# Mixture-of-experts stage: another order of issue for the transposes and evictions of the gated values

## The chip, the cores and the metric

The kernel runs on one core of a Trainium2 chip. The metric is the device time of one execution in microseconds. A measurement is the median of several runs; the trace is one profiled execution of the same program.

## What is computed

The reference is a two-layer transformer with mixers, one dense SwiGLU layer and, at the end, a mixture of 8 experts over 256 tokens of width 1024. The change lies in the mixture alone:

```python
def swiglu(h, w1, w3, w2):
    return (jax.nn.silu(h @ w1) * (h @ w3)) @ w2

def moe_swiglu(h, w_router, w1, w3, w2):
    logits = jnp.einsum('bnd,de->bne', h, w_router).astype(jnp.float32)
    top_vals, top_idx = lax.top_k(logits, TOP_K)          # 2 of 8
    gates = jax.nn.softmax(top_vals, axis=-1)
    ...
    for e in range(N_EXPERTS):
        out = out + combine[..., e:e + 1].astype(h.dtype) * swiglu(h, w1[e], w3[e], w2[e])
    return out
```

`w1[e]` and `w3[e]` are 1024 x 3584, `w2[e]` is 3584 x 1024, all in float32.

## The kernel before, in words

Experts are ordered by how many tokens they got. Even places (`small_(e)` false) are called big and take up to 128 tokens, odd ones small and take up to 64. An expert's 3584 inner columns are cut into 7 blocks of 512. The list `seq` orders the (expert, block) steps; but for its head and one stretch after the first big expert it alternates a big step and a small step, and such two together are called a **pair** here.

A float32 weight is not multiplied as it is. ScalarE copies a piece of 128 x 1024 into a rounded half `whi` (line 75), VectorE subtracts it into `wlo` (line 76), and TensorE multiplies both. These two instructions are a **split**; there are six buffers for split pieces, and `W.take()` prepares splits so far ahead that six are ready or in use. So the split of a piece can start when TensorE is done with the piece six places earlier. One quarter of a small step's `w1` and of its `w3` is used unsplit (line 1434).

Step i does the following:

- `hidden(p1, e)` and `hidden(p3, e)` multiply the tokens by the block of `w1` and of `w3`, four pieces each. For a big step (lines 1446 to 1448) the pieces are called **B1 to B4** (p1) and **B5 to B8** (p3) below, 6 matmuls each. For a small step (line 1438, 4 matmuls a piece) they are **S1 to S3** and **S4 to S6**, with the unsplit quarter behind S2 and behind S5.
- Between the two halves `turn(i - 1, prev, ...)` transposes the values of the step before: for a big one 4 transposes of `sl` (line 1477, called **T4**), then `gh` on ScalarE and `gl` on VectorE from PSUM; for a small one 8 transposes of two tiles `c` (line 1459, **T8**), then two `u` copies on ScalarE (1463), two `u` sums on VectorE (1464), Silu (1465), the product (1466), and the halves of `g`.
- After the second half, the values of this step leave PSUM: big, Silu on ScalarE and a product on VectorE into `sl` (1547, 1548); small, two copies `c` on ScalarE (1544).
- `finish(i - 1)` multiplies the turned values of the step before by four pieces of `w2`: **F1 to F4** for a small one (line 1493, 4 matmuls each), **G1 to G4** for a big one (line 1497, 6 each).

So a pair uses 22 split pieces in the order B1 to B8, F1 to F4, S1 to S6, G1 to G4, and the transfers of twelve raw tiles of 1024 KB, which SP issues in a ring of twelve. When an expert's last block is done, `rows` and `scatter` put its result back: products `po` into PSUM (1514, 1515), each evicted by VectorE into `xl` (line 400).

The order of each engine's queue is made by a scheduler, which lists what it thinks is ready sooner first. `tc.issue_after(m)` adds an edge without a wait: what is traced in its block goes behind m in the queue of the same engine. Before the change, the only such edges here are on the transposes: behind the sixth step of eight of the first half for a big step, behind the fourth for a small one (`TURN = (5, 3)`). They are traced after the whole half, and the copies and products have no edge.

Of the kernel before, what the change touches and what calls it, by code (L numbers as in the profile page):

```python
# [12 lines left out]
F32 = mybir.dt.float32  # L13
# [4 lines left out]
ALU = mybir.AluOpType  # L18
# [11 lines left out]
NF = EDIM // 512  # L30
EPS = 1e-6
RAW, RAW0, RAWF, RAW2, RAW3, WS, WS2 = 4, 5, 3, 5, 3, 3, 3
TURN = (5, 3)
FK = 7
KY = (2, 6)
QN = 4
# [11 lines left out]
def program(ctx, tc, a, out, upto=99, tap=None):  # L48
    nc = tc.nc
    V, S, G, TE = nc.vector, nc.scalar, nc.gpsimd, nc.tensor  # L50
# [21 lines left out]

    def split(hi, lo, full, eng=None):

        S.copy(hi, full)  # L75
        (eng or V).tensor_tensor(lo, full, hi.bitcast(F32), op=ALU.subtract)  # L76

    def mm3(o, wh, wl, xh, xl, first, last, **kw):
        TE.matmul(o, wh, xh, start=first, stop=False, **kw)  # L79
# [39 lines left out]
    class Stream:  # L119
# [20 lines left out]
        def prepare(self, n):  # L140
            while sum(lo is not None for _, lo in self.split_) < n and (self.ready or self.todo):
                self.fetch()
                t, whole = self.ready.popleft()
                if whole:
                    self.split_.append((t, None))
                    continue
                p = pairs.pop(0)
                pairs.append(p)
                hi = p.tile([P, 1024], F32R, tag="whi", name="whi")
                lo = p.tile([P, 1024], F32R, tag="wlo", name="wlo")  # L150
                split(hi, lo, t)
                self.split_.append((hi, lo))

        def take(self, ahead=None):
            ahead = self.ahead if ahead is None else ahead
# [3 lines left out]
    W = Stream(1)  # L159
# [7 lines left out]
    def small_(e):  # L167
        return e % 2 == 1
# [298 lines left out]
    with ExitStack() as st:  # L467
# [87 lines left out]
        u = mix.tile([P, 8], F32, name="u")  # L555
# [170 lines left out]
        po = bank("po")  # L726
# [693 lines left out]
    def experts(x0, then=None):  # L1420

        xg, py, gTs = {}, {}, {}

        def hidden(po, e):
            ms = []
            for q in range(4):
                wh, wl = W.take()
                if small_(e):
                    xs_, xf = (xg[e][n] for n in "sf")
                    for k2 in range(2):  # L1430
                        kt = 2 * q + k2
                        w = slice(512 * k2, 512 * (k2 + 1))
                        if wl is None:
                            m = TE.matmul(po[0:64], xf[:, kt], wh[:, w], start=False, stop=False, skip_group_check=True)  # L1434
                        else:
                            x_ = xs_[:, kt].rearrange("p u s -> p (u s)")
                            for z in (wh, wl):
                                m = TE.matmul(po, x_, z[:, w], start=kt == 0 and z is wh,  # L1438
                                              stop=kt == KT - 1 and z is wl, skip_group_check=True)
                        ms.append(m)  # L1440
                    continue
                xh, xl = xg[e]["h"], xg[e]["l"]
                for k2 in range(2):
                    kt = 2 * q + k2
                    w = slice(512 * k2, 512 * (k2 + 1))
                    TE.matmul(po, xh[:, kt], wh[:, w], start=kt == 0, stop=False)  # L1446
                    TE.matmul(po, xh[:, kt], wl[:, w], start=False, stop=False)  # L1447
                    m = TE.matmul(po, xl[:, kt], wh[:, w], start=False, stop=kt == KT - 1)  # L1448
                    ms.append(m)
            return ms  # L1450

        def turn_small(i, cs, m=None):

            pts = []
            with tc.issue_after(m.ins) if m else ExitStack():
                for c in cs:
                    pt = bank("pt")
                    for k in range(4):
                        TE.transpose(pt[:, P * k:P * (k + 1)], c[:, P * k:P * (k + 1)], ident)
                    pts.append(pt.rearrange("p (k u s) -> p k u s", k=4, u=2))  # L1460
            u = t512("u").rearrange("p (n k s) -> p n k s", n=2, k=4)
            for n, pt in enumerate(pts):
                S.copy(u[:, n], pt[:, :, 1])
                V.tensor_tensor(u[:, n], pt[:, :, 0], u[:, n], op=ALU.add)
            S.activation(u[:, 0], u[:, 0], AF.Silu)
            V.tensor_mul(u[:, 0], u[:, 0], u[:, 1])
            gT = t512("g").bitcast(F32R).rearrange("p (k u s) -> p k u s", k=4, u=2)
            split(gT[:, :, 0], gT[:, :, 1], u[:, 0])
            gTs[i] = gT

        def turn(i, sl, m=None):
            if small_(seq[i][0]):
                return turn_small(i, sl, m)
            pt = bank("pt")
            with tc.issue_after(getattr(m, "ins", m)) if m else ExitStack():
                for k in range(4):
                    TE.transpose(pt[:, P * k:P * (k + 1)], sl[:, P * k:P * (k + 1)], ident)
            gT = {n: t512(f"g{n}").bitcast(F32R).rearrange("p (k s) -> p k s", k=4) for n in "hl"}
            split(gT["h"], gT["l"], pt.rearrange("p (k s) -> p k s", k=4))
            gTs[i] = gT  # L1480

        def finish(i):
# [39 lines left out]
        prev = done = None  # L1522
        for i, (e, f) in enumerate(seq):
            p1, p3 = bank("p1"), bank("p3")
            ms = hidden(p1, e)
            if i == 0 and then:
                then()
            if i == QN:
                queue.clear()
            if i == 2 and not ids:  # L1530
                for j in range(1, EXP):
                    k = HP * (j % 2) + j // 2
                    ids[j] = nc.values_load(ords[0:1, k:k + 1].bitcast(I32), engines=[mybir.EngineType.SP],
                                            min_val=0, max_val=EXP - 1)
            if prev is not None:
                turn(i - 1, prev, ms[TURN[small_(e)]])
            if done:
                scatter(*done)
                done = None
            hidden(p3, e)  # L1540
            if small_(e):
                prev = [t512("c") for _ in range(2)]
                for c, po in zip(prev, (p1, p3)):
                    S.copy(c, po)  # L1544
            else:
                prev = t512("sl")
                S.activation(prev, p1, AF.Silu)
                V.tensor_mul(prev, prev, p3)
            if i == 0:
                one_hots(1)  # L1550
            if i == 1:
                xg[1] = gather(1)
            if f == NF - 1 and e < EXP - 2:
                xg[e + 2] = gather(e + 2)
            if i == len(seq) - 1:
                turn(i, prev)
            if i:
                finish(i - 1)
                if seq[i - 1][1] == NF - 1:
                    done = seq[i - 1][0], rows(seq[i - 1][0])  # L1560
            if f == 3 and e % 2 == 0:
                slots_back(e // 2)
            if f == 4 and e < EXP - 2:
                one_hots(e + 2)
# [108 lines left out]
```

## Time and profile before

| | us |
|---|---|
| median of 3 runs | 1800.47 (1798.79 to 1802.83) |
| profiled execution | 1802.29 |
| its span, first to last instruction | 1800.5 |
| TensorE busy | 1741.5 (97%) |
| VectorE busy | 1444.6 (80%) |
| ScalarE busy | 1039.4 (58%) |

The expert stage is about the second half of the span. Busy matmuls overlap each other in this profile, so TensorE's 97% does not say that it runs at its peak; distances between starts do. Where a row says what an engine waited for, that is the instruction whose end came last. A wait of an engine that is ahead costs nothing; what counts is where TensorE waits.

### The profile page before, as it was taken

The page shows a single profiled execution, that of the slowest core. Times are in us where ns is not written, and L with a number is a line of the kernel's source. Part 1 is how long each engine was busy: PE and PEld are TensorE (multiplying, and loading weights), DVE is VectorE, ACT ScalarE, POOL GpSimd, SP SyncE. Part 2 cuts the span into 40 slices and gives each one's busy share as a digit, 9 for nine tenths or more (in the row PEclk, how much of TensorE's full clock was granted, in tenths as well). Part 3 has the DMA queues.
Part 4 walks back from the last instruction along what each step waited for, and adds up shares of the span by engine and source line. Part 5 has one row for each costly group of instructions (what it writes and reads, how often), then busy time and mean ns, then how long its engine had stood idle before and what let it go on. Part 6 is the DMA issues. An engine that isn't in the chain of part 4 may idle for free.

```text
span 1800.5 us, 24070 instructions
## 1 busy us (share of the span) xinstructions
PE 1741.5 (97%) x8672; PEld 1365.1 (76%) x8672; DVE 1444.6 (80%) x2369; ACT 1039.4 (58%) x1425; POOL 7.4 (0%) x10
## 2 busy tenths in 40 slices
PE   6999999999999999999999999999999999999997
PEld 4778888888888899987777776766776777777675
DVE  5566599987554988877898888888888888988887
ACT  3353342222223455556787776777767777767775
POOL 0000000000000000000000000000000000000000
PEclk9999999999999999997999999999999999999999
DMA  8543554755212221176999899999989999899990
GB/s 364 187 165 121 228 211 178 276 201 192 112 54 88 94 71 71 52 292 237 351 374 402 349 327 359 394 362 383 364 310 361 373 391 369 326 365 378 378 387 34
DMA packets 65935, 474.12 MB, mean 263 GB/s; under 512 B 7312, under 2 KB 7696, under 8 KB 8464
## 3 DMA queue, kind: packets, MB, share of 16 engines
q1 hardware_dynamic: 65664, 472.31, 69.1%
q8 instruction: 70, 1.15, 0.3%
q14 instruction: 57, 0.47, 0.1%
q10 hardware_dynamic: 144, 0.20, 0.0%
HBM read 471.43 MB, written 1.05 MB: 262 GB/s over the span
## 4 chain that ended last, share of the span: by engine, by line
PE 80%; DVE 10%; ACT 4%; issue 4%; DMA 2%; DVEq 0%; SPq 0%; ACTq 0%
PE p L1438 9%; PE py L1497 8%; DVE wlo L76 6%; PE p L1434 5%; PE p L80 4%; PE p L81 4%; PE p L79 4%; PE p L1446 4%; PE p L1447 4%; PE p L1448 4%; PE po L79 3%; PE po L80 3%; PE po L81 3%; PE py L1493 3%; ACT whi L75 3%
## 5 line engine op out<-in xcount | busy, mean ns | idle before, releaser
L76 DVE TENSOR_TENSOR wlo<-raw,whi 128x1024 fp32r<-128x1024 f32 x738 | 873.0, 1221 | 142.9 <-ACT whi L75 133.8
L75 ACT CAST whi<-raw 128x1024 fp32r<-128x1024 f32 x738 | 741.8, 1049 | 365.4 <-PE p L80 157.4
L1446 PE MATMUL p<-whi,xh 128*128 128x512 f32 x448 | 178.0, 397 | 0.0
L1447 PE MATMUL p<-wlo,xh 128*128 128x512 f32 x448 | 175.5, 392 | 0.0
L1448 PE MATMUL p<-whi,xl 128*128 128x512 f32 x448 | 175.2, 391 | 0.0
L1438 PE MATMUL p<-whi,xs 128*128 128x512 f32 x336 | 141.6, 422 | 1.6 <-ACT c L1544 1.5
L1438 PE MATMUL p<-wlo,xs 128*128 128x512 f32 x336 | 136.7, 407 | 5.0 <-DVE wlo L76 5.0
L80 PE MATMUL p<-hlo,whi 128*128 128x512 f32 (+1 forms) x368 | 139.7, 381 | 0.2
L79 PE MATMUL p<-hhi,whi 128*128 128x512 f32 (+1 forms) x368 | 138.3, 381 | 1.1 <-ACT hhi L363 1.1
L81 PE MATMUL p<-hhi,wlo 128*128 128x512 f32 (+1 forms) x368 | 139.3, 380 | 0.0
L1434 PE MATMUL p<-raw,xf 128*64 128x512 f32 x224 | 108.1, 605 | 0.0
L1438 PEld LDWEIGHTS p<-whi,xs 128*128 128x128 f32 x336 | 63.7, 189 | 57.8 <-ACT whi L75 22.1
L1447 PEld LDWEIGHTS p<-wlo,xh 128*128 128x128 f32 x448 | 84.8, 189 | 18.3
L1446 PEld LDWEIGHTS p<-whi,xh 128*128 128x128 f32 x448 | 84.9, 190 | 17.3 <-ACT xh L75 0.2
L1448 PEld LDWEIGHTS p<-whi,xl 128*128 128x128 f32 x448 | 84.7, 189 | 17.5
L1497 PE MATMUL py<-wlo,gh 128*128 128x512 f32 x224 | 88.6, 396 | 0.1
L1497 PE MATMUL py<-whi,gl 128*128 128x512 f32 x224 | 88.7, 396 | 0.0
L1493 PE MATMUL py<-wlo,g 128*128 128x512 f32 x224 | 84.8, 411 | 3.7 <-DVE wlo L76 3.7
L1493 PE MATMUL py<-whi,g 128*128 128x512 f32 x224 | 83.9, 407 | 2.4 <-DVE g L76 0.9
L1438 PEld LDWEIGHTS p<-wlo,xs 128*128 128x128 f32 x336 | 63.8, 190 | 28.6 <-DVE wlo L76 18.6
L941 PE MATMUL pp<-wlo,hhi 128*128 128x256 f32 x288 | 81.8, 284 | 1.2 <-DVE wlo L76 1.2
L940 PE MATMUL pp<-whi,hhi 128*128 128x256 f32 x288 | 82.6, 287 | 0.0
(373 smaller groups left out, 3205.1 us busy)
## 6 DMA issues: line engine op xcount, KB each, us to landing
raw<-moe_w SPq DMA_DIRECT2D x335, 1024.0 KB, 7.3
raw<-ffn SPq DMA_DIRECT2D x33, 1024.0 KB, 4.9
raw<-w_mod SPq DMA_DIRECT2D x24, 1024.0 KB, 7.3
raw<-w_mod_t SPq DMA_DIRECT2D x24, 1024.0 KB, 4.9
raw<-w_in_odd SPq DMA_DIRECT2D x12, 1024.0 KB, 4.7
raw<-w_in_even SPq DMA_DIRECT2D x6, 1024.0 KB, 6.7
raw<-w_out_even SPq DMA_DIRECT2D x4, 1024.0 KB, 7.0
raw<-w_out_odd SPq DMA_DIRECT2D x4, 1024.0 KB, 4.8
```

Source lines behind the costliest of these rows:

```text
L75: S.copy(hi, full)
L76: (eng or V).tensor_tensor(lo, full, hi.bitcast(F32), op=ALU.subtract)
L79: TE.matmul(o, wh, xh, start=first, stop=False, **kw)
L80: TE.matmul(o, wh, xl, start=False, stop=False, **kw)
L81: TE.matmul(o, wl, xh, start=False, stop=last, **kw)
L1434: m = TE.matmul(po[0:64], xf[:, kt], wh[:, w], start=False, stop=False, skip_group_check=True)
L1438: m = TE.matmul(po, x_, z[:, w], start=kt == 0 and z is wh, stop=kt == KT - 1 and z is wl, skip_group_check=True)
L1446: TE.matmul(po, xh[:, kt], wh[:, w], start=kt == 0, stop=False)
L1447: TE.matmul(po, xh[:, kt], wl[:, w], start=False, stop=False)
L1448: m = TE.matmul(po, xl[:, kt], wh[:, w], start=False, stop=kt == KT - 1)
L1493: TE.matmul(py[e][n], gT[:, ft].rearrange("p u s -> p (u s)"), w[:, 512 * n:512 * (n + 1)], start=first and w is wh, stop=last and w is wl)
L1497: TE.matmul(py[e][n], gT[g][:, ft], w[:, 512 * n:512 * (n + 1)], start=first and g == "h" and w is wh, stop=last and g == "l")
```

## The change

Three things in the source. (1) The transposes are traced inside the first half, right behind its fourth step of eight (the end of its second quarter), for big and small steps alike: `TURN = 3`. (2) The `Stream` of weights remembers the two instructions of the split that it prepared last (`W.last`), and `W.then(k)` puts what follows behind it on ScalarE (k = 0) or VectorE (k = 1). (3) That is used for the `u` copies and sums, `gh` and `gl`, both `c` copies and the product `sl`. No instruction is added or taken away.

```diff
-TURN = (5, 3)
+TURN = 3
     def split(hi, lo, full, eng=None):
-        S.copy(hi, full)
-        (eng or V).tensor_tensor(lo, full, hi.bitcast(F32), op=ALU.subtract)
+        h = S.copy(hi, full)
+        return h, (eng or V).tensor_tensor(lo, full, hi.bitcast(F32), op=ALU.subtract)
...
-                split(hi, lo, t)
+                self.last = split(hi, lo, t)
...
+        def then(self, i=0):
+
+            return tc.issue_after(self.last[i].ins)
...
-        def hidden(po, e):
-            ms = []
+        def hidden(po, e, at=None):
...
-                    ms.append(m)
-            return ms
+                    if kt == TURN and at:
+                        at(m)
...
-                S.copy(u[:, n], pt[:, :, 1])
-                V.tensor_tensor(u[:, n], pt[:, :, 0], u[:, n], op=ALU.add)
+                with W.then():
+                    S.copy(u[:, n], pt[:, :, 1])
+                with W.then(1):
+                    V.tensor_tensor(u[:, n], pt[:, :, 0], u[:, n], op=ALU.add)
...
-            split(gT["h"], gT["l"], pt.rearrange("p (k s) -> p k s", k=4))
+            pv = pt.rearrange("p (k s) -> p k s", k=4)
+            with W.then():
+                S.copy(gT["h"], pv)
+            with W.then(1):
+                V.tensor_tensor(gT["l"], pv, gT["h"].bitcast(F32), op=ALU.subtract)
...
-            ms = hidden(p1, e)
+            hidden(p1, e, None if prev is None else lambda m: turn(i - 1, prev, m))
...
-            if prev is not None:
-                turn(i - 1, prev, ms[TURN[small_(e)]])
...
-                    S.copy(c, po)
+                    with W.then():
+                        S.copy(c, po)
...
-                V.tensor_mul(prev, prev, p3)
+                with W.then(1):
+                    V.tensor_mul(prev, prev, p3)
```

What it moves is told by the order of the built programs. ScalarE's queue before, in a pair in the middle of expert 2's blocks: the first row ends with the splits of B1 to B6, and the row under it is the two `u` copies.

```order
L75 CAST whi<-raw 128x1024 x8
L1463 COPY u<-pt 128x256 x2
L75 CAST whi<-raw 128x1024 x2
L1465 ACTIVATE u<-u 128x256
L75 CAST whi<-raw 128x1024
L75 CAST g<-u 128x4x64
L75 CAST whi<-raw 128x1024
L1547 ACTIVATE sl<-p_10914 128x512
L75 CAST whi<-raw 128x1024 x7
L75 CAST gh<-pt 128x512
L75 CAST whi<-raw 128x1024
L1544 COPY c<-p_11065 128x512
```

The same pair now (the lines of the new file are some four to twelve higher): the `c` copies stand behind B1, the `u` copies behind B7, `gh` behind G1.

```order
L1553 COPY c<-p_10795 128x512
L1553 COPY c<-p_10796 128x512
L75 CAST whi<-raw 128x1024 x6
L1468 COPY u<-pt 128x256 x2
L75 CAST whi<-raw 128x1024
L1471 ACTIVATE u<-u 128x256
L75 CAST whi<-raw 128x1024 x2
L75 CAST g<-u 128x4x64
L1556 ACTIVATE sl<-p_10914 128x512
L75 CAST whi<-raw 128x1024 x9
L1487 CAST gh<-pt 128x512
L75 CAST whi<-raw 128x1024 x4
```

Of the split rows, x2 became x1 ahead of Silu and x7 plus one became x9 ahead of `gh`. On TensorE T8 moved from behind B4 to behind B2 in all such pairs, and T4 from behind the first half of the small step to behind S2. On VectorE `sl` moved from behind F2 to behind S1.

One pair of the program before has another order than its neighbours, that of the second block of expert 4 (its T8 starts at 1347.04 us in the trace). On ScalarE the seven splits of its second row are B2 to B8, and the `u` copies stand behind them:

```order
L1544 COPY c<-p_12017 128x512
L75 CAST whi<-raw 128x1024 x7
L1463 COPY u<-pt 128x256 x2
L75 CAST whi<-raw 128x1024
L1465 ACTIVATE u<-u 128x256
L75 CAST whi<-raw 128x1024
L75 CAST g<-u 128x4x64
```

In this one the change leaves the `u` copies where they are, behind B8.

The program's end, on ScalarE before: behind the last small step's two `c` copies come its `u` copies (its T8 stands right behind S6 on TensorE, cut in two by three matmuls of G1).

```order
L1544 COPY c<-p_15745 128x512
L75 CAST whi<-raw 128x1024 x2
L1544 COPY c<-p_15746 128x512
L1463 COPY u<-pt 128x256 x2
L75 CAST whi<-raw 128x1024 x2
L1465 ACTIVATE u<-u 128x256
L75 CAST whi<-raw 128x1024
L75 CAST g<-u 128x4x64
```

The same place now; on TensorE the last T8 stands behind all matmuls of G1 to G4, and two splits and the Silu stand behind the `u` copies here.

```order
L1553 COPY c<-p_15745 128x512
L1553 COPY c<-p_15746 128x512
L75 CAST whi<-raw 128x1024
L1468 COPY u<-pt 128x256 x2
L75 CAST whi<-raw 128x1024 x2
L1471 ACTIVATE u<-u 128x256
L75 CAST g<-u 128x4x64
```

The last split of all stood behind `g` and now stands ahead of the Silu.

## Rows read from the trace of the kernel before

**Rows 1.** Chain that ended last, in time: start us, us, what.
```profile
1122.36 5.47 PE py L1497 x24
```

**Rows 2.** TensorE's timeline, T8 and T4: start us, us, engine, line, operation, count.
```profile
895.68 1.03 PE L1459 MATMUL pt<-const,c 128*128 128x128 f32 x8
...
928.50 1.03 PE L1459 MATMUL pt<-const,c 128*128 128x128 f32 x8
...
1100.15 1.03 PE L1459 MATMUL pt<-const,c 128*128 128x128 f32 x8
...
1266.12 1.04 PE L1459 MATMUL pt<-const,c 128*128 128x128 f32 x8
...
1347.04 1.03 PE L1459 MATMUL pt<-const,c 128*128 128x128 f32 x8
...
1362.01 0.60 PE L1477 MATMUL pt<-const,sl 128*128 128x128 f32 x4
...
1378.19 1.03 PE L1459 MATMUL pt<-const,c 128*128 128x128 f32 x8
...
1511.18 1.04 PE L1459 MATMUL pt<-const,c 128*128 128x128 f32 x8
...
1620.32 1.03 PE L1459 MATMUL pt<-const,c 128*128 128x128 f32 x8
...
1752.52 1.04 PE L1459 MATMUL pt<-const,c 128*128 128x128 f32 x8
...
1769.28 0.60 PE L1477 MATMUL pt<-const,sl 128*128 128x128 f32 x4
```

**Rows 3.** ScalarE's timeline in one pair; in brackets the idle time before, and its releaser.
```profile
1133.76 0.81 ACT L1463 COPY u<-pt 128x256 f32<-128x256 f32 x2 [3.19 <-PE pt L1459]
...
1140.03 6.73 ACT L75 CAST whi<-raw 128x1024 fp32r<-128x1024 f32 x7
1150.52 0.59 ACT L75 CAST gh<-pt 128x512 fp32r<-128x512 f32 x1 [3.76 <-PE pt L1477]
```

**Rows 4.** Waits from 800 us on: who waited for whom, us, times, longest.
```profile
ACT u L1463 <- PE pt L1459: 65.0, 25, 3.8
...
ACT whi L75 <- DMA raw<-moe_w: 0.6, 2, 0.3
```

**Rows 5.** VectorE's timeline in the same pair.
```profile
1134.16 0.86 DVE L1464 TENSOR_TENSOR u<-pt,u 128x256 f32<-128x256 f32 x2 [1.02 <-ACT u L1463]
...
1140.82 0.68 DVE L1548 TENSOR_TENSOR sl<-sl,p 128x512 f32<-128x512 f32 x1
1141.42 8.03 DVE L76 TENSOR_TENSOR wlo<-raw,whi 128x1024 fp32r<-128x1024 f32 x7
```

**Rows 6.** TensorE's timeline in the same pair.
```profile
1144.96 0.50 PE L1438 MATMUL p<-wlo,xs 128*128 128x512 f32 x1 [0.17 <-DVE wlo L76]
...
1149.88 0.60 PE L1477 MATMUL pt<-const,sl 128*128 128x128 f32 x4
```

**Rows 7.** TensorE's timeline where a result is put back.
```profile
1029.84 0.39 PE L1514 MATMUL po<-pT,yh 128*128 128x256 f32 x1 [1.50 <-ACT c L1544]
...
1554.62 0.39 PE L1514 MATMUL po<-pT,yh 128*128 128x256 f32 x1 [1.40 <-DVE xl L400]
```

**Rows 8.** Timelines of TensorE and VectorE at the end.
```profile
1774.56 0.60 PE L1459 MATMUL pt<-const,c 128*128 128x128 f32 x4
...
1781.43 0.42 DVE L76 TENSOR_TENSOR g<-u,g 128x256 fp32r<-128x256 f32 x1
```

**Rows 9.** Windows: busy us of each engine (instructions), TensorE's clock, transfer share, GB/s.
```profile
980.00:1000.00 20.00, 20.00 (x105) 17.03 (x104) 16.94 (x19) 15.64 (x19) 0.00 (x0) 1.00 1.01 417
...
1100.00:1200.00 100.00, 97.71 (x410) 69.11 (x409) 85.42 (x90) 73.98 (x91) 0.00 (x0) 1.00 0.98 376
```

More of the change, by code (lines that the diff above doesn't have):

```diff
@@ L1448, in hidden @@
                     m = TE.matmul(po, xl[:, kt], wh[:, w], start=False, stop=kt == KT - 1)
-                    ms.append(m)
-            return ms
+                    if kt == TURN and at:
+                        at(m)
         def turn_small(i, cs, m=None):
```

## The prediction, made before the changed kernel was timed

> **What bounds the kernel now.** I began with the page's shares, then asked who waits for whom in the expert stage (860 to 1800 us of the span), then laid the three engines' instructions of one pair of steps side by side in time. TensorE is the engine to follow: its 24 matmuls of a second product take 5.47 us [rows 1], that is 0.228 us each with nothing between them, so a quarter of a big half (6 matmuls) is 1.37 us and a quarter of a small step (4) is 0.91 us.
>
> The period of a pair is the distance from one group of eight transposes (of a small step's values; T8 below) to the next [rows 2]. From 1100.15 to 1266.12 five pairs take 165.97 us, from 1378.19 to 1511.18 four take 132.99, from 1620.32 to 1752.52 four take 132.20: about 33.0 each. But from 1347.04 to 1378.19 one takes 31.15, with the same instructions. So about 1.8 us of a pair is waiting, and it is not lost in every pair. That is what a change of order can win.
>
> Where it goes: ScalarE, in order, stands 3.19 us at the `u` copy until the transposes come, and 3.76 us at `gh` [rows 3]; in all it waits 65.0 us for T8 at the line of `u` [rows 4]. VectorE, which makes the second half of each split from ScalarE's first, stands behind it (1.02 us before its `u`) and then runs seven splits without a pause, 8.03 us or 1.15 each [rows 5]; in that stretch TensorE has caught up and waits for a `wlo` [rows 6]. The one unhurried pair differs in just this: in its order the `u` copies stand behind B8, in the slow ones behind B6 (both are shown with the change). Weights are not what is waited for: ScalarE waited 0.6 us in all for a weight transfer [rows 4].
>
> **The change, part by part.** The instructions are the same in number and kind on every engine, and SP's queue of transfers is the same, so only waits can move. I clock a pair from TensorE's first matmul of B1 = 0, all six split buffers full.
>
> (a) T8 goes from behind B4 to behind B2, and the `u` copies from behind the split of B6 to that of B7. TensorE: B1 and B2 to 2.73, T8 (1.03 us [rows 2]) to 3.8, B3 to 5.1, B4 to 6.5, B5 to B8 to 11.95, F1 to F4 to 15.6, S1 and S2 to 17.4. A split may begin when the piece six places earlier has been used. B7's buffer is free at 1.37, so its first half is done at 2.4. A copy follows its transposes' start by 0.64 us (1149.88 to 1150.52 [rows 3, 6]): the two `u` copies run from 3.4 to 4.2. ScalarE's wait there is about 1.0 us instead of 3.19. Then the splits by VectorE's 1.15 us, ScalarE's 0.96 (6.73 for seven [rows 3]) before them: B8 ready 6.4, product of `u` 6.8, F1 7.95, `g` 8.4, F2 9.5, F3 10.7, F4 11.8, S1 13.0 (its buffer comes free at 10.6). TensorE wants F1 and `g` at 11.95, F4 at 14.7, S1 at 15.6: everything is 2.5 us or more ahead, where before it was late.
>
> (b) `sl` moves behind S1's split on VectorE and T4 (the four transposes of a big step) ahead of the unsplit quarter: `sl` (0.68 us [rows 5]) ends at 13.7, S2 at 14.8; TensorE reaches S2 at 16.5 and T4 at 17.4. T4 stands in TensorE's own queue, so whatever `sl` lacks is paid there in full; the spare is 3.7 us.
>
> (c) `gh` moves behind G1 and both `c` copies behind the next B1. `gh` still waits for T4, but G1 to G4 are not wanted for another 8 us. The `c` copies wait for the end of S6, which the buffer of B2 waits for as well, so they add only their own time to a queue that is 4 us ahead. I put (c) at nothing; without that cover it would be 2 times 0.6 us a pair.
>
> The sum for steady pairs, at the unhurried period of 31.15: 165.97 - 5 x 31.15 = 10.22, 132.99 - 4 x 31.15 = 8.39, 132.20 - 4 x 31.15 = 7.60. Each run holds one pair with extra work on routing (transposes of `hot`), which a pair with the same extra shows as 928.50 - 895.68 = 32.82, so 1.67 comes off each: 8.55 + 6.72 + 5.93 = 21.2. The last pair's T8 to T4 is 16.76 against 14.97 in the unhurried one [rows 2]: 1.8. **Steady pairs: -23.0.** Bounds: 0 if the wait only changes places, -23 if all of it goes (the period cannot be shorter than the 31.15 by order alone, as far as rows show).
>
> (d) Where one expert's result is put back. At 1029.84 TensorE waits 1.50 for a `c` copy to free a PSUM bank [rows 7]; the new order puts five of the `xl` evictions ahead of the `u` work there, and the small step's second product no longer stands ahead of a half. I take -2 there. At the two later places (1.40 at 1554.62 [rows 7]) the evictions still stand behind `g`, and now all eight in a row: +0.5 each. Bounds for the three together: -4.5 (all such waits gone) to +4 (one more wait of 1.4 at each).
>
> (e) The end. The last T8 stood right behind S6; the order now has it behind all 24 matmuls of G1 to G4, 5.47 us later, with two splits and then the Silu behind the `u` copies. From S6's end (1774.56): 5.47 + 0.64 + 0.81 (copies) + 2 x 0.96 + 0.42 (Silu, taken as one more step like `g`) + 0.42 (product) + 1.15 (last split) + 0.42 (`g`) = 11.3; before, `g` ended at 1781.85, that is 7.3 [rows 8]. What follows (16 matmuls, sixteen evictions) was interleaved with three splits that are then already done, about 1 us. **+3**, bounds 0 (copies find cover) and +5.5 (the whole of G1 to G4).
>
> Sum: -23.0 - 2 + 1 + 3 = -21. The profiled execution took 1802.29 us, the span 1800.5 of it; so 1781.3 for it, and from the median of the three runs, 1800.47, which lies 1.8 below, **1779.5 us**.
>
> **A rule against it.** Twelve transfers of 1024 KB (12.58 MB) feed a pair. At 31.15 us that asks for 404 GB/s. The rows show 376 GB/s at a transfer share of 0.98 over 1100 to 1200, and 417 at 1.01 over 980 to 1000 [rows 9].
>
> The Trainium skill, "DMA: Bandwidth & Descriptors", section Where 436 GB/s comes from, gives about 358 GB/s as the limit of memory for one core and 435 for the ports, and says that for transfers from memory the 358 binds. By it no pair could be under 35.1 us and nothing would be won (1800 and a tail of 3). The trace disagrees, with 417 GB/s in [rows 9] and a pair of 31.15 us in [rows 2].
>
> **Rivals.** (1) *The weights become the bound.* For it: a share of 0.98 to 1.01. Against it: 417 GB/s over 20 us, and no waiting for weights in the row above. If the stage cannot hold more than 390 GB/s (half way between the 376 of the rows and the 404 asked for), a pair stays at 32.3 us, 0.7 x 14 = 10 us are won, less the 2 that (d) and (e) add: 1792. (2) *ScalarE's wait shrinks but does not go*, since the `u` copies move by a single split and still meet their transposes late. Half of 23 is left: -11.5 + 2, also 1791. For it: the one unhurried pair had them two splits later. Against it: T8 comes two quarters earlier as well. (3) *More goes than the steady waits*: the waits of (d) at all places, the end covered: -23 - 4.5 - 3 (the waits in the first pairs of an expert that I left out), about 1770. (4) *Slower: T4 comes too early.* Were VectorE to gain nothing, `sl` would end at 1140.82 + 0.68 + 3 x 1.15 = 1144.95, and T4 would stand some 4.6 us before 1149.88 (2.8 us of matmuls that it passes, 1.8 of waits), at 1145.3: a spare of 0.3 us. From there each microsecond by which VectorE is later is paid on TensorE in each of some 25 pairs: one split late (1.15) makes 0.85 x 25 = 21, with the end's 3, 1824. It decides from 0.3 us on; my clocking has 3.7.
>
> **How the numbers follow.** Forecast 0.64 (its own range 1774 to 1786, from the bounds of (d) and (e)); rival 1 0.12, rival 2 0.09, rival 3 0.09, rival 4 0.06. The range of 8 in 10 takes in rivals 1 to 3 and leaves out rival 4 and the far ends: 1770 to 1793. A measurement of this kernel can tell about 0.2% (3.6 us) from no change. Faster by more than that: the forecast, rival 3 and nearly all of rivals 1 and 2, 0.88; within it: the low ends of rivals 1 and 2, 0.05; slower: rival 4 and a little of (d), 0.07.
>
> **What would show it.** The distance between T8 groups is 31 to 31.5 in all steady pairs; ScalarE's wait at the `u` copy is near 1 us, its total a third of 65.0; VectorE's stretches without a pause no longer end in TensorE waiting for a `wlo`; T4 waits for nothing; the end from S6 on is about 3 us longer. It is wrong if T8 to T8 stays near 33 (which wait ends there tells rival 1, a transfer, from rival 2, a ScalarE copy), or if TensorE waits before T4 for `sl`.

## The result, and the profile after

The changed kernel took 1781.29 us (median of 4 runs, 1780.00 to 1783.31), the kernel before 1799.63 beside it: ratio 0.9893, 95% interval 0.9881 to 0.9906. Predicted were 1779.5. The profiled execution took 1780.0 us, its span is 1778.1.

Busy times of the page after: us, share of the span, instructions.

```profile
PE 1720.7 (97%) x8672; PEld 1373.6 (77%) x8672; DVE 1440.7 (81%) x2369; ACT 1050.1 (59%) x1425; POOL 7.4 (0%) x10
```

TensorE's share is 97% as before, though its busy time fell by 21 us, from 1741.5: the share said nothing about where the time was. TensorE's timeline does, by the starts of T8 (start us, us, engine, line, operation, count), as [rows 2] before. The first two are neighbours in the middle of expert 2, the other two lie around a putting back.

```profile
1090.64 1.03 PE L1463 MATMUL pt<-const,c 128*128 128x128 f32 x8
1121.59 1.03 PE L1463 MATMUL pt<-const,c 128*128 128x128 f32 x8
...
1286.47 1.03 PE L1463 MATMUL pt<-const,c 128*128 128x128 f32 x8
1329.65 1.03 PE L1463 MATMUL pt<-const,c 128*128 128x128 f32 x8
```

The pair is 30.95 us where it was 32.97. ScalarE's and VectorE's timelines of the same pair, as [rows 3, 5] (in brackets the idle time ahead and its releaser):

```profile
1122.22 0.81 ACT L1468 COPY u<-pt 128x256 f32<-128x256 f32 x2 [0.74 <-PE pt L1463]
...
1136.73 0.58 ACT L1487 CAST gh<-pt 128x512 fp32r<-128x512 f32 x1
...
1144.54 0.59 ACT L1553 COPY c<-p 128x512 f32<-128x512 f32 x1 [1.63 <-PE p L1441]
```

```profile
1127.20 4.65 DVE L76 TENSOR_TENSOR wlo<-raw,whi 128x1024 fp32r<-128x1024 f32 x4
1131.77 0.68 DVE L1558 TENSOR_TENSOR sl<-sl,p 128x512 f32<-128x512 f32 x1
1132.36 6.90 DVE L76 TENSOR_TENSOR wlo<-raw,whi 128x1024 fp32r<-128x1024 f32 x6
```

The wait at `u` is 0.74 us (before 3.19), that at `gh` is gone (before 3.76). In TensorE's timeline F1 to F4 now follow each other at 0.91 us a piece, S1 comes right behind them, and T4 stands there without a wait, 3.65 us after `sl` has ended (1131.77 + 0.68):

```profile
1130.65 0.39 PE L1503 MATMUL py<-whi,g 128*128 128x512 f32 x1
...
1134.28 0.39 PE L1441 MATMUL p<-whi,xs 128*128 128x512 f32 x1
...
1136.10 0.60 PE L1483 MATMUL pt<-const,sl 128*128 128x128 f32 x4
```

In such a pair no matmul has an idle time ahead of it any more: 30.95 us is what TensorE's own work takes at this order. Who waited for whom from 800 us on (us, times, longest), as [rows 4], and a window of two pairs (its length, busy us of PE, PEld, DVE, ACT, POOL, then clock, transfer share, GB/s), as [rows 9]:

```profile
ACT u L1468 <- PE pt L1463: 17.0, 18, 4.4
...
ACT whi L75 <- DMA raw<-moe_w: 1.5, 5, 0.3
```

```profile
1090.64:1152.54 61.90, 61.90 (x266) 46.24 (x264) 57.83 (x59) 50.33 (x60) 0.00 (x0) 1.00 1.00 408
```

The transfers kept up: 408 GB/s over 62 us, and 1.5 us of waiting for a weight in all. The rule that the prediction weighed (the Trainium skill, "DMA: Bandwidth & Descriptors", section Where 436 GB/s comes from) has about 358 GB/s as what binds transfers from memory; this row, with 408, disagrees.

Laid end to end by the starts of T8, the two traces give this (us; T8 is two quarters, 2.73 us, earlier in its pair now, which the first row gains and the last gives back):

| stretch | before | after | change | predicted |
|---|---|---|---|---|
| start to first T8 | 895.68 | 892.90 | -2.78 | -2.73 |
| three pairs, first expert | 95.50 | 94.23 | -1.27 | 0 |
| first putting back, with two neighbours | 108.97 | 103.51 | -5.46 | -2 |
| five pairs | 165.97 | 157.66 | -8.31 | -8.55 |
| second putting back | 80.92 | 81.35 | +0.43 | +0.5 |
| five pairs | 164.14 | 157.70 | -6.44 | -6.72 |
| third putting back | 77.98 | 81.09 | +3.11 | +0.5 |
| five pairs | 163.36 | 156.94 | -6.42 | -5.93 |
| last pair and end | 47.98 | 52.72 | +4.74 | +2.73 - 1.8 + 3 |
| span | 1800.5 | 1778.1 | -22.4 | -21 |

### The profile page after: what moved, and what is told of

It reads as the page before. It is cut to its first block, busy times and chain, and to the rows that moved or that the text cites. A ratio compares the mean times of both kernels' runs of the same rounds, so it can differ in the third digit from the quotient of the medians.

```text
span 1778.1 us, 24106 instructions
## 1 busy us (share of the span) xinstructions
PE 1720.7 (97%) x8672; PEld 1373.6 (77%) x8672; DVE 1440.7 (81%) x2369; ACT 1050.1 (59%) x1425; POOL 7.4 (0%) x10
## 3 DMA queue, kind: packets, MB, share of 16 engines
q8 instruction: 70, 1.15, 0.3%
## 4 chain that ended last, share of the span: by engine, by line
PE 90%; DVE 6%; ACT 1%; DMA 1%; issue 1%; SPq 0%; DVEq 0%; ACTq 0%
PE p L1441 9%; PE py L1507 9%; PE p L1437 6%; PE p L1450 5%; PE p L1451 5%; PE p L1452 5%; PE py L1503 5%; PE p L80 4%; PE p L81 4%; PE p L79 4%; PE po L79 3%; PE po L80 3%; PE po L81 3%; PE pg L1407 2%; DVE wlo L76 2%; PE pp L945 2%
## 5 line engine op out<-in xcount | busy, mean ns | idle before, releaser
L75 ACT CAST whi<-raw 128x1024 fp32r<-128x1024 f32 x738 | 752.1, 1050 | 427.2 <-PE p L80 157.4
L946 PE MATMUL pp<-whi,hlo 128*128 128x256 f32 x288 | 81.5, 283 | 0.0
L1503 PE MATMUL py<-wlo,g 128*128 128x512 f32 x224 | 81.2, 395 | 0.0
```

The source lines that it names most:

```text
L75: h = S.copy(hi, full)
L1503: TE.matmul(py[e][n], gT[:, ft].rearrange("p u s -> p (u s)"), w[:, 512 * n:512 * (n + 1)], start=first and w is wh, stop=last and w is wl)
```

## The experiments

Three ideas stood against each other. **D**, distance: an engine's queue runs in order, so a copy that waits for its transposes holds up the splits behind it, and what counts is how many splits stand in ScalarE's queue between the place of T8 and the copy; I call these the pieces **ready** at T8 (before: T8 behind B4, `u` behind B6, so 2; now T8 behind B2, `u` behind B7, so 5). **P**, place: the earlier transposes are the gain. **Rivals on cost**: which of the moved instructions carries it, or whether too few buffers or the weights do. The steady pair is the measure, since it repeats to about 0.1 us within a kernel (one pair of 32.26 in e6 aside); the medians also hold what happens where a result is put back, and the clock there.

| kernel | T8, `u` behind | ready | `sl` behind | steady pair, us | median, us |
|---|---|---|---|---|---|
| before | B4, B6 | 2 | F2 | 32.97 | 1799.5 to 1800.8 |
| e1, transposes alone | B2, B4 | 2 | F2 | 32.93 | 1795.40 |
| e8, seven buffers | B4, B6 | 2 | F2 | 32.92 | 1800.82 |
| e4, all edges but `u` | B2, B4 and B6 | 2 | S1 | 32.53 | 1805.41 |
| e3, `u` edges alone | B2, B7 | 5 | F2 | 32.02 | 1785.96 |
| e6, no edges on `c`, `sl` | B2, B7 | 5 | F2 | 31.88 | 1783.88 |
| e2, edges alone | B4, B8 | 4 | S1 | 31.14 | 1788.66 |
| e5, no edges on `gh`, `gl` | B2, B7 | 5 | S1 | 31.08 | 1785.15 |
| e9, no edges on `c` | B2, B7 | 5 | S1 | 31.05 | 1768.56 |
| e10, TURN = 1 | B1, B6 | 5 | S1 | 30.97 | 1779.54 |
| e11, TURN = 7 | B4, F1 | 5 | S1 | 30.97 | 1783.35 |
| changed kernel | B2, B7 | 5 | S1 | 30.95 | 1781.29 |

### Place or distance: e1, e2, e11, e10

e1 takes every `with W.then(...)` away and keeps the transposes where the change has them:

```diff
-                with W.then():
+                with ExitStack():
                     S.copy(u[:, n], pt[:, :, 1])
```

(and so at the other edges).

> Part (1) alone: the transposes stand where the change puts them (T8 behind B2, T4 behind S2), no copy or product has an edge. The scheduler answers by moving the copies along: `u` behind the split of B4 (before: B6, changed kernel: B7), `gh` behind S4. So each copy stands as near behind its transposes as before. Theory D (what counts is how many splits stand ahead of a copy in ScalarE's queue after its transposes are asked for, so that ScalarE has work until they come): nothing is won, pairs of 33.0 us (32.6 to 33.4), ScalarE's wait at `u` 55 to 75 us in all, 1800 (1794 to 1806). Theory P (the earlier place of the transposes is the gain, since `u`, `g` and F1 start earlier): pairs near 31, 1781 (1777 to 1786).

Measured: 1795.40, ratio 0.997 (0.9956 to 0.9984), pairs of 32.93, ScalarE's wait at `u` 46.0 us in all (theory D had 55 to 75). **The earlier transposes alone win nothing in a steady pair.** The 5 us that it is faster lie elsewhere: the first putting back takes 104.35 us, before 108.97, and most of that is the clock, whose mean there is 1.00 and was 0.97.

e2 is the reverse: `TURN = (5, 3)`, the turn traced behind the whole half as before, with the split that the half had prepared at its fourth step as the edge.

> Parts (2) and (3) alone: edges on the same splits as in the changed kernel, the transposes where they were before (T8 behind B4, T4 behind the first half of the small step). The scheduler then has `u` behind B8 (the order of the one unhurried pair of the kernel before), `gh` behind G2, `c` behind B1. Theory D: the gain is there without any move of the transposes: pairs of 31.0 us (30.9 to 31.4), wait at `u` under 30 us in all, 1781 (1776 to 1788). Theory P: pairs near 33, 1800 (1794 to 1806).

Measured: 1788.66, ratio 0.9925 (0.9898 to 0.9952), just above the range that D had (1788 at most); the pair is as D said. ScalarE's wait at `u` is not: 43.8 us in all where D had under 30, 2.10 in a steady pair, and the pair hardly pays for it. TensorE's timeline:

```profile
1101.27 1.03 PE L1463 MATMUL pt<-const,c 128*128 128x128 f32 x8
...
1132.41 1.03 PE L1463 MATMUL pt<-const,c 128*128 128x128 f32 x8
```

31.14 us with T8 in its old place: that is the 31.15 of the unhurried pair of [rows 2]. What it lacks beside the changed kernel lies in the steady stretches (478.5 against 472.3 us, half of it in the pairs with extra work, two of 34.8 and one of 34.6 against two of 33.9 and one of 33.1) and at the first putting back (107.91 against 103.51).

e11 and e10 change one number, `TURN`, to 7 and to 1.

> The changed kernel with the transposes as late as the kernel before had them: TURN = 7, T8 behind B4 and T4 behind the first half of the small step. The edges follow and put `u` behind F1 and `gh` behind G2. Theory D: five pieces are ready at T8 again, so pairs of 31.0 us (30.9 to 31.2) with T8 in its old place, unless the last half of `g` comes too late for F1 (clocked: `g` 0.5 to 1 us ahead of it, so a loss of up to 0.5 a pair is open: 31.4). 1781 to 1789. Theory P (place): 33.0, 1800.

> The changed kernel with the transposes one more quarter earlier: TURN = 1, so T8 stands behind B1 and T4 behind S1; the edges follow (`u` behind B6, `gh` behind S6). Theory D: five pieces stay ready at T8, as with TURN = 3, and `sl` has 3.7 us of spare in the changed kernel, of which a quarter of the small half takes 0.9: pairs of 30.95 (30.9 to 31.2), 1781 (1777 to 1786). The prediction's rival 4 (T4 too early, TensorE waits for `sl`): each pair 0.5 us or more longer, 1793 or more.

Measured: 1783.35, ratio 0.9898 (0.9874 to 0.9921), and 1779.54, ratio 0.987 (0.9842 to 0.9899). T8 of e11, at its old place behind B4, and its `u` copies behind F1 in ScalarE's timeline:

```profile
1098.97 1.03 PE L1463 MATMUL pt<-const,c 128*128 128x128 f32 x8
...
1129.94 1.03 PE L1463 MATMUL pt<-const,c 128*128 128x128 f32 x8
```

```profile
1130.57 0.81 ACT L1468 COPY u<-pt 128x256 f32<-128x256 f32 x2 [0.74 <-PE pt L1463]
```

30.97 us, and the same 0.74 us of wait at `u` as in the changed kernel. T8 behind B1, B2 or B4 gives the same pair as long as five pieces are ready. **Place is out, distance stands.**

The kernel before shows the same inside one trace. Counted there, its hurried pairs all have 2 pieces ready. The unhurried one at 1347.04 has 4, and there is a second like it, at 1589.16, also with 4, which takes 31.17 us; the pairs at 928.50 and 959.82 have 6 and take 31.32 and 31.36. e10 also tells that T4 a quarter earlier still finds `sl` done: the prediction's rival 4 has more room than the trace of before could show.

### Buffers or order: e8

```diff
-RAW, RAW0, RAWF, RAW2, RAW3, WS, WS2 = 4, 5, 3, 5, 3, 3, 3
+RAW, RAW0, RAWF, RAW2, RAW3, WS, WS2 = 4, 5, 3, 5, 2, 3, 4
```

in the kernel before.

> The kernel before, its order untouched (`u` behind B6, `gh` behind S5, T8 behind B4), with seven split buffers instead of six and eleven raw tiles instead of twelve. Theory D (the copy's place in ScalarE's queue sets how far ahead VectorE is at T8: B6 is ready and B7 is not, whatever the number of buffers): pairs stay at 32.97 (32.7 to 33.2), 1800 (1795 to 1804). Rival L (six buffers are too few, and the change only hides that): pairs fall to 31 to 32, 1785 (1778 to 1793). Rival W (the ring of weights is tight): pairs grow past 33.3, 1806 or more.

Measured: 1800.82, ratio 1.001 (0.9997 to 1.0024). T8, and ScalarE at `u`:

```profile
1094.74 1.04 PE L1459 MATMUL pt<-const,c 128*128 128x128 f32 x8
...
1127.66 1.04 PE L1459 MATMUL pt<-const,c 128*128 128x128 f32 x8
```

```profile
1128.30 0.81 ACT L1463 COPY u<-pt 128x256 f32<-128x256 f32 x2 [3.18 <-PE pt L1459]
```

32.92 us, and ScalarE stands 3.18 us at `u` (before 3.19), although a seventh buffer is there for the split behind it. **More buffers do not help where the order of the queue holds the work back.** The run changes two things, one buffer more and one raw tile less, but the unchanged wait at `u` says that no gain of the one is hidden by the other. Its two pairs with 6 pieces ready (T8 at 1343.10 and 1586.80) take 30.99 us. The Trainium skill ("PSUM — Partial Sum Buffer", section Engine vs sequencer instructions) calls the queues of ScalarE and VectorE strictly first in, first out; the 3.18 us of the row above agree.

The size can be clocked now, from the rows of before: T8 on TensorE, and the splits behind the `u` sums on VectorE.

```profile
1133.12 1.04 PE L1459 MATMUL pt<-const,c 128*128 128x128 f32 x8
...
1135.55 2.36 DVE L76 TENSOR_TENSOR wlo<-raw,whi 128x1024 fp32r<-128x1024 f32 x2 [0.52 <-ACT whi L75]
```

With 2 pieces ready, VectorE ends the `u` sums 1.9 us after T8's start (1134.16 + 0.86 in [rows 5], less 1133.12) and waits 0.5 for the next first half. From there to S2 it has eight splits of 1.15 (B7 to S2), two steps of `u` and `g` at 0.34 from start to start, and `sl` at 0.60: 10.5, so S2 is ready 12.9 us after T8's start. TensorE wants it after 0.79 + 5.47 + 3.64 + 0.91 = 10.8 (T8, B5 to B8, F1 to F4, S1). That is 2.1 us late; measured 32.97 - 30.95 = 2.02. With 4 ready two splits fall away, 2.3 us, and nothing is late; measured 0.19. This clocking has no wait at `sl`; the next runs show one as soon as `u` has been moved without it.

### Which moved instruction: e3 to e6, e9

> The changed kernel with the edges on the `u` copies and sums alone; `gh`, `gl`, `c` and the product `sl` are free, and the scheduler has `gh` behind S4 again (before: S5, changed: G1). Theory D in the form that the wait at `u` carries the gain and the wait at `gh` is covered (the prediction's (c)): `gh` waits 50 to 70 us in all again, and pairs are still 31.0 (30.9 to 31.5), 1782 (1777 to 1788). Theory H (both waits cost about alike, since before ScalarE stood 65.0 us at `u` and 68.4 at `gh`): pairs of 32 (31.7 to 32.4), 1791 (1787 to 1796).

Measured: 1785.96, ratio 0.9918 (0.9886 to 0.995), pairs of 32.02: half, as theory H said (the median lies in D's range and below H's), and `gh` waited 64.1 us. I took that to be `gh`'s doing. It was not.

> The opposite: edges on all but the `u` copies and sums. The scheduler has one `u` copy behind B4 and one behind B6, with T8 behind B2. Theory D with the wait at `u` as the carrier: no more than a small part of the gain, pairs of 32.5 to 33.2, 1797 (1791 to 1803). Theory H: half, 32 and 1791. Theory P: 31 and 1781.

Measured: 1805.41, ratio 1.0014 (0.9993 to 1.0034): unchanged at best and above what any of the three theories gave, though the pair is a little shorter (32.53, in D's range). ScalarE waits 87.1 us at `u`. Its pairs with extra work are longer, 35.1 against 34.1, so that the steady stretches win 1 us in all, and the last pair and end take 57.18 us (before 47.98, and 2.73 for the place of T8).

> The changed kernel without the edges on `gh` and `gl` alone: the scheduler has `gh` behind S4 again (as in e3), all else as in the changed kernel. After e3 the theory is: a copy that stands k splits behind the place of its transposes in TensorE's order lets VectorE be no more than k pieces ahead there, and what it lacks is paid in F1 to S2, where TensorE takes 0.91 us a piece and VectorE makes one in 1.15. Theory G (in e3 it was `gh` behind S4 that cost 1.1 us a pair): pairs of 32.0 us again (31.8 to 32.2), `gh` waits over 55 us in all; 1785 (1781 to 1790). Theory C (it was the product `sl` and the `c` copies): pairs of 30.95, 1779 (1775 to 1784).

Measured: 1785.15, ratio 0.9911 (0.9891 to 0.993). Its waits:

```profile
ACT gh L1487 <- PE pt L1483: 57.8, 17, 4.2
ACT u L1468 <- PE pt L1463: 16.7, 19, 3.8
```

`gh` waits 57.8 us in all (before 68.4), up to 4.2 at a time, and the pair is 31.08: **those waits cost 0.13 us a pair.** (In the traces of e1, e3 and e5 `gh` stands behind S3 in the steady pairs, one piece earlier than the expectations say; the median is a little above theory C's range.) I read it so: behind `gh` VectorE has the whole of G1 to G4 and B1 to B4, at 1.37 us a piece for TensorE against 1.15, to make it good. Theory G fell, and with it my reading of e3.

> The changed kernel without the edges on the `c` copies and the product `sl`: `gh` stays behind G1, the `c` copies go behind G2, `sl` behind F2. Theory G: pairs of 30.95 (30.9 to 31.1), 1781 (1777 to 1785). Theory C: pairs of 32.0, 1790 (1785 to 1795).

Measured: 1783.88, ratio 0.9901 (0.9884 to 0.9918), pairs of 31.88: by the pair, though not by the median, it is `c` or `sl`. e9 tells them apart, with `sl` kept on its edge:

```diff
                 for c, po in zip(prev, (p1, p3)):
-                    with W.then():
+                    with ExitStack():
                         S.copy(c, po)
```

> The changed kernel without the edges on the two `c` copies alone; `sl` keeps its own. ScalarE has both `c` copies behind G2 (changed kernel: behind the next B1), and the order where a result is put back becomes that of e6. Theory C now says: the second `c` copy waits for the end of S6 with only G1 and G2 split, and the pieces that are then late cannot all be made good until S2: pairs of 31.9 us (31.7 to 32.1), as in e6, and the second pair at each of the two later places of putting back 39.1 instead of 43: 1783 (1779 to 1787). Rival S (it was `sl` that stood too early on VectorE in e6): pairs of 30.95, 1772 (1768 to 1776).

Measured: 1768.56, ratio 0.9824 (0.98 to 0.9849), pairs of 31.05. My theory C was wrong, the rival right. VectorE's timeline of the same pair, e6 first, then e9:

```profile
1130.86 0.69 DVE L1558 TENSOR_TENSOR sl<-sl,p 128x512 f32<-128x512 f32 x1 [0.74 <-PE p L1452]
```

```profile
1132.48 0.67 DVE L1558 TENSOR_TENSOR sl<-sl,p 128x512 f32<-128x512 f32 x1
```

In e6 `sl` stands behind F2's split and VectorE waits 0.74 us for the last matmul of B8, with the splits that TensorE wants next behind it in the queue; in e9 it stands behind S1 and waits for nothing. The pairs differ by 0.83 us. In the kernel before `sl` had no wait ahead of it in [rows 5]: there `u` made VectorE late already, and this second wait showed only when the first was gone. The `c` copies, on the other hand, waited 106.5 us in all in e9 and cost 0.1 a pair.

### Where a result is put back, and the end: e7, e12

In the changed kernel TensorE loses time where the small expert's result is put back (its timeline; then windows with the clock in the column behind POOL):

```profile
1532.24 0.39 PE L1524 MATMUL po<-pT,yh 128*128 128x256 f32 x1 [1.75 <-ACT sl L1556]
...
1552.32 0.36 PE L1524 MATMUL po<-pT,yh 128*128 128x256 f32 x1 [1.23 <-DVE gl L1489]
...
1553.76 0.66 PE L1441 MATMUL p<-whi,xs 128*128 128x512 f32 x1 [0.96 <-DVE xl L404]
```

```profile
1530.00:1540.00 10.00, 8.21 (x34) 6.57 (x33) 8.34 (x15) 4.90 (x6) 0.00 (x0) 0.83 0.70 239
1550.00:1560.00 10.00, 7.81 (x27) 4.67 (x26) 9.46 (x15) 2.87 (x4) 0.00 (x0) 0.83 0.71 281
```

The waits of 1.23 (for `gl`, which frees the bank of its transposes) and 0.96 (for an eviction) are new against [rows 7], and behind the waits of both windows the clock falls: the mean of 0.83 is a third of the window at 1.2 GHz instead of 2.4. e7 took the edges off `gh` and `gl` in these steps, and off the last step's `c` and `u` copies.

> The changed kernel with two places mended: no edges on `gh` and `gl` in the four steps in which a result is put back (there `gl` stands a split and an eviction earlier again and frees its PSUM bank sooner), and none on the `c` and `u` copies of the last step (T8 stands inside G1 again). Theory: steady pairs stay at 30.95; the end from the last full pair on is 2 to 3 us shorter (52.7 to about 50); the pairs with the second putting-back (43.2 and 42.9 us) fall by 1.5 to 4 each, since the waits of 1.23 for `gl` and 0.96 for `xl` go with the low clock behind them: 1773 (1769 to 1777). Rival: the wait only moves to the evictions, which now stand behind two splits; then only the end is won, 1779 (1777 to 1781).

Measured: 1776.54, ratio 0.9864 (0.9844 to 0.9884). The end did as expected and more, 48.75 us against 52.72. At the putting back the rival was right: the two pairs stayed at 42.99 and 42.94, and TensorE's wait only changed its releaser:

```profile
1553.65 0.38 PE L1524 MATMUL po<-pT,yh 128*128 128x256 f32 x1 [2.16 <-DVE xl L404]
```

e6 and e9 had shown another way: without the edges on `c` the scheduler puts three evictions, not one, ahead of G1's split there. T8 around the second putting back in e9:

```profile
1284.88 1.03 PE L1463 MATMUL pt<-const,c 128*128 128x128 f32 x8
...
1322.45 1.03 PE L1463 MATMUL pt<-const,c 128*128 128x128 f32 x8
```

37.57 us, in the changed kernel 43.18 (1329.65 - 1286.47). The two stretches as windows, the changed kernel first, then e9:

```profile
1286.47:1329.65 43.18, 39.11 (x165) 29.48 (x164) 38.36 (x51) 27.95 (x34) 0.00 (x0) 0.92 0.80 290
```

```profile
1284.88:1322.45 37.57, 35.50 (x166) 27.20 (x164) 37.05 (x50) 27.86 (x34) 0.00 (x0) 1.00 0.85 310
```

Of the 5.6 us some 3.4 (0.08 of 43.18, an estimate) are the clock; the rest fits the waits for `gl` and the eviction there, 1.32 and 0.96 us in the changed kernel. e12 keeps the changed kernel and drops only these edges:

```diff
-                with W.then():
+                with W.then() if m else ExitStack():
                     S.copy(u[:, n], pt[:, :, 1])
-                with W.then(1):
+                with W.then(1) if m else ExitStack():
                     V.tensor_tensor(u[:, n], pt[:, :, 0], u[:, n], op=ALU.add)
...
-            p1, p3 = bank("p1"), bank("p3")
+            back = done; p1, p3 = bank("p1"), bank("p3")
...
-                    with W.then():
+                    with ExitStack() if (back or f == NF - 1) and i > 20 else W.then():
                         S.copy(c, po)
```

> The changed kernel with two places mended on other grounds than in e7: no edge on the `u` copies of the last step, and none on the `c` copies in an expert's last small step and in the small step in which a result is put back, at the two later places (steps 27, 29, 41, 43) and the end (55). Steady pairs stay at 30.95, the pairs with the second putting-back fall from 43.2 and 42.9 to 39.1 as in e6 (7.9 us in all), a pair or two ahead of them cost up to 1 us more, the end is 4 us shorter as in e7: 1770 (1767 to 1773). Rival: the low clock behind TensorE's waits comes at other places instead, 1777 as in e7.

Measured: **1765.76 us** (1765.52 to 1766.72), ratio 0.9805 (0.9783 to 0.9828), the best of all and below my range. Steady pairs 30.94; the two pairs of the putting back 37.03 and 37.56 (I had taken 39.1 from e6, in which `sl` still stood at F2), both with a mean clock of 1.00; last pair and end 49.27.

## Why the prediction was right, point by point

- **The bound and its size.** Right. The steady stretches were to give -8.55, -6.72 and -5.93, together -21.2; they gave -8.31, -6.44 and -6.42, together -21.2. The unhurried pair was a fair measure of what order alone can reach: 31.15 taken, 30.95 measured. The pairs with extra work are 33.9, 33.9 and 33.1 and not 32.8, which ate up the difference; that the two misses cancel to a tenth is luck. In each of these VectorE now stands behind a small copy of the routing work:

```profile
1163.05 0.16 DVE L1387 COPY gs<-pg 128x2 f32<-128x2 f32 x1 [3.69 <-PE pg L1385]
```

  e11 waits 0.95 there and has these pairs at 32.34, but e10 waits 0.83 and has 34.60; so some 1.5 us of each can be won by order, and what decides it is open.
- **(a), `u`.** Right in mechanism: the wait fell from 3.19 to 0.74 us (about 1.0 clocked), its total from 65.0 to 17.0 (a third was expected), and e1, e2, e8 and e11 show that the number of splits ahead of the copy does it, not the place of T8 that I put first in (a). By itself (e3 against e1) it is worth 0.91 us a pair.
- **(b), `sl` and T4.** The spare was clocked at 3.7 and is 3.65. But I saw in the move of `sl` only a risk. e9 against e6 shows that it carries 0.83 of the 2.02 us: without it the wait at `u` would have been followed by one at `sl`. The sum came out, since I measured by the whole pair; its reason was incomplete. I wrote that the unhurried pair differs from the hurried ones in just the place of `u`. It differs in more: on VectorE its `sl` stands behind F4, two splits later than the F2 of the others.

```profile
1352.94 2.36 DVE L76 TENSOR_TENSOR wlo<-raw,whi 128x1024 fp32r<-128x1024 f32 x2 [0.44 <-ACT whi L75]
1355.21 0.68 DVE L1548 TENSOR_TENSOR sl<-sl,p 128x512 f32<-128x512 f32 x1
```

  (The two splits are F3 and F4.) Its 31.15 held both gains, and the change happened to make both moves.
- **(c), `gh` and `c` at nothing.** Right: 0.13 (e5) and 0.1 (e9) a pair, though `gh` had the largest total of waits in the trace of before.
- **(d), putting back: -2 + 0.5 + 0.5 taken, -5.46 + 0.43 + 3.11 measured.** The sum is near (-1.0, -1.9) by luck, the terms are not. I priced the waits and left out the clock. The three stretches as windows, before:

```profile
991.18:1100.15 108.97, 106.98 (x473) 77.67 (x472) 93.77 (x114) 77.64 (x105) 0.00 (x0) 0.97 0.90 338
1266.12:1347.04 80.92, 77.80 (x361) 59.69 (x360) 72.37 (x91) 59.23 (x78) 0.00 (x0) 0.96 0.89 328
1511.18:1589.16 77.98, 74.82 (x362) 57.30 (x361) 71.91 (x91) 59.05 (x78) 0.00 (x0) 1.00 0.92 340
```

  and in the changed kernel:

```profile
987.13:1090.64 103.51, 102.44 (x473) 76.03 (x472) 93.06 (x115) 80.23 (x108) 0.00 (x0) 1.00 0.94 359
1248.30:1329.65 81.35, 77.28 (x361) 59.74 (x360) 69.78 (x89) 56.93 (x76) 0.00 (x0) 0.96 0.87 330
1487.35:1568.44 81.09, 77.11 (x361) 59.59 (x360) 69.75 (x89) 57.26 (x76) 0.00 (x0) 0.96 0.88 330
```

  The clock won some 3.3 us at the first place, cost some 3.2 at the third, and was the same at the second (estimates: what the mean lacks to 1.00, times the stretch). Without it about -2, +0.4 and 0 are left, near what I took. The eight evictions in a row, which I had as the loss, cost little: at the third place T8 to T4 took 19.59 us before (1550.06 to 1569.65) and takes 20.33 now (1525.52 to 1545.85; both groups moved up by about as much), with a fall of the clock in it. The new waits are for `gl` and the eviction behind it, 20 us later.
- **(e), the end: +3 taken.** `g` was to be done 11.3 us after S6; it is at 11.05 (1758.76 + 0.42, from 1753.60 - 5.47). What follows did not get 1 us shorter: from S6 to the end it is 29.97 us against 25.94, +4.0, within the bounds of 0 and 5.5. In part that is the clock again: behind TensorE's wait of 4.15 us matmuls stand 0.43 apart, not 0.23:

```profile
1758.79 0.80 PE L1524 MATMUL po<-pT,yh 128*128 128x256 f32 x2 [4.15 <-ACT yh L1514]
...
1760.25 0.63 PE L1503 MATMUL py<-whi,g 128*128 128x512 f32 x1
1760.68 0.63 PE L1503 MATMUL py<-wlo,g 128*128 128x512 f32 x1
```

- **First pairs, left out:** -1.27, some 0.4 us each.
- **Rivals.** Weights as the bound: no, 408 GB/s. Half a wait left: no, 0.74 us. T4 too early: no, not even a quarter earlier (e10).

## What to carry to other kernels

In an in-order queue ask of every instruction that waits for another engine how many pieces of work stand ahead of it, counted from the place where what it waits for is issued; five held here, two cost 0.9 us a pair by themselves and 2.0 together with the wait at `sl`, and neither an earlier producer (e1) nor another buffer (e8) makes up for it. The total of waits does not rank them: 68 us at `gh` were nearly free (as I read it, since a stretch of slower consumption lay behind them), and a wait of 0.74 us at `sl` that no trace of before showed was worth 0.83 a pair. Edges that are right in the steady loop should be looked at again at its seams: dropping them there gave another 15.5 us (1781.29 to 1765.76), of which an estimated 5 are the clock (3.4 less at each of the two later places of putting back, 1.6 more in the pair ahead of one of them).

## What the runs showed of the hardware

Waits of TensorE where a result is put back are often followed by a stretch at the lower of its two clocks, 1.2 GHz, which costs nearly as much again (about 1.6 us each time). But the wait's length alone does not tell: in the changed kernel 1.75 us at 1532.24 was followed by it, in e9 2.07 us at 1291.92 was not, as its timeline and windows show.

```profile
1291.92 0.38 PE L1524 MATMUL po<-pT,yh 128*128 128x256 f32 x1 [2.07 <-ACT sl L1556]
```

```profile
1285.00:1295.00 10.00, 7.93 (x47) 6.83 (x46) 10.00 (x19) 7.21 (x11) 0.00 (x0) 1.00 0.85 304
1295.00:1305.00 10.00, 10.00 (x45) 7.79 (x45) 9.48 (x10) 7.40 (x8) 0.00 (x0) 1.00 0.74 256
```

Nor does it take a wait that the profile shows. From T8 to T8 ahead of the second putting back (1247.16 to 1286.90 in e7, 1248.30 to 1286.47 in the changed kernel) TensorE, VectorE and ScalarE have the same instructions in the same order in both traces. TensorE is busy throughout in both windows, e7 first, and yet in e7 the clock falls and the stretch is 1.57 us longer:

```profile
1270.00:1290.00 20.00, 20.00 (x98) 15.71 (x97) 14.70 (x19) 14.16 (x23) 0.00 (x0) 0.91 0.89 344
```

```profile
1271.14:1291.14 20.00, 20.00 (x109) 16.02 (x108) 16.18 (x22) 15.51 (x25) 0.00 (x0) 1.00 0.93 354
```

So one such stretch can come and go with the order unchanged, and a difference of 1.6 us at one place between two traces is not yet the order's. Whole executions say so too: the mean clock of the changed kernel's four is 0.984 or 0.986, that of the kernel before 0.985 to 0.989, and one such stretch makes 0.001 of it (1.6 of 1780 us). The steady pairs of the changed kernel, at a clock of 1.00 in the window of two pairs above, are free of this. What decides it stays open; no run here separates it.
